# Forgetting attention: one exp over a tile's logits in SBUF, in place, and four PSUM banks for logits in place of two

## The chip, the cores and the metric

The kernel runs on one core of a Trainium2 chip. A core has a matrix engine (PE, which reads SBUF and writes PSUM only), a vector engine (DVE), a scalar engine (ACT), GpSimd (POOL) and a queue that issues DMAs (SP). Each engine takes its instructions in order, and they meet at semaphores. The metric is the device time of one execution, in microseconds. Three runs of the kernel before took 1284.34, 1287.81 and 1289.43 us, the median is 1287.81.

## The reference

Two layers over a sequence of 1024 tokens of 1024 channels. Layer 0 mixes by causal pooling and layer 1 by forgetting attention; both add an attention into 256 memory tokens, gates and an output projection with a layer norm. The part that is changed is the forgetting attention, 16 heads of 64 channels:

```python
logits = einsum('bqhd,bkhd->bhqk', q, k) * 64 ** -0.5
logits = logits + (cum[t] - cum[s])      # cum: running sum of log forget gates
logits = where(s <= t, logits, -inf)
p = softmax(logits, axis=-1)
out = einsum('bhqk,bkhd->bqhd', p, v)
```

`cum[t]` is the same for a whole row, so it cancels in the softmax, and only `cum[s]` has to be added.

## The kernel before, in words

Matrix products that need more precision than one pass of PE gives are made of two or three passes over a high and a low part of each operand. `slab` (line 171) is the workhorse: 128 output channels by 1024 tokens, 48 matmuls of 512 columns into two of three PSUM banks with the tag `pj`, evacuated by ACT and DVE. Its weights come by DMA and are split in two by ACT and DVE, or, while `low[0]` is set, as it is in the forgetting attention, by POOL (lines 146 and 147).

PSUM has eight banks: one for value products (tag `O`), three for slabs (`pj`), two for logits (`L`) and two for transposes (`T`). In the forgetting attention the two `T` banks hold exps.

The forgetting attention is `fox` (line 759). PE's order there is the order of the program text (a manual schedule for PE alone); a scheduler sets the order on DVE, ACT, POOL and SP. For each of the 16 heads it goes through eight tiles of 128 queries, the longest first: tile i has L = 128 (i + 1) keys, in two parts of up to 512 keys where L is over 512, and in one part otherwise. Between a tile's own products PE is given a share of other work, `fill.pump`: the slabs of the next pair of heads and of the gates. One step does this for tile i, the tile before it and the tile five steps back (`LAG`):

- `probs` (line 673): POOL masks the diagonal block of R, the broadcast row of `cum` (line 682, in place; R is loaded once a head). Per part, PE makes two logits passes into an `L` bank (line 688, recorded as line 169), and DVE adds R, writes the result to the tile `p` in SBUF (tag `MK`, four buffers, shared with the value projections) and carries the running minimum along (line 689, a custom instruction and a read of its accumulator). q is stored negated, so the minimum is the softmax's maximum.
- then `behind()` runs `halves` (line 701) of the tile before: DVE adds the parts' sums of exps and scales them (line 706; line 708 for one part) and takes the reciprocal (line 709); per part, ACT writes the high half of the probabilities as fp16 (line 712), and DVE the low half, exp times r less the high half (line 713).
- then the rest of `probs`: per part, ACT takes the exp of `p` into a `T` bank, with its sum (line 695, an ACTIVATE and an accumulator read).
- `turn` (line 718) transposes the halves by a DMA from SP, and five steps later `values` (line 724) multiplies them with the values; ACT and DVE evacuate (lines 738 and 739).

Other work on the same engines in this stage: queries and keys are evacuated by ACT and DVE (lines 627, 628, 638, 639), gates by lines 194 and 195, values by lines 236 to 244, the finished heads are gated by POOL (lines 748 and 756), and in the last pair of heads the output projection's weights are split by ACT and DVE (lines 142 and 143).

Of the kernel before, what the change touches and what calls it, by code (L numbers as in the profile page):

```python
# [9 lines left out]
F32 = mybir.dt.float32  # L10
# [4 lines left out]
AF = mybir.ActivationFunctionType  # L15
ALU = mybir.AluOpType
AX = mybir.AxisListType

P = 128
# [3 lines left out]
ST = S // P  # L23
NH = 512
# [13 lines left out]
PSCALE = 2.0 ** 15  # L38
# [27 lines left out]
def run(units):  # L66
    for _ in units:
        pass
# [3 lines left out]
def trunk_kernel(ctx, tc, x, xT, memT, win, wk, wv0, wv, wmk, wmv, wout, poolw, pscale, lng, lnb, bforget, out):  # L72
# [5 lines left out]
    nc = tc.nc  # L78
# [3 lines left out]
    small = ctx.enter_context(tc.tile_pool(name="small", bufs=4))  # L82
    psum = ctx.enter_context(tc.tile_pool(name="psum", bufs=2, space=bass.MemoryType.PSUM))
# [1 line left out]
        nc.vector.memset(small.tile([P, 8], F32, tag="edge", name="edge"), 0.0)  # L85
    dram = ctx.enter_context(tc.tile_pool(name="dram", bufs=1, space=bass.MemoryType.DRAM))

    count, low = [0], [False]
    since = [0]
    warm = pool.tile([P, NH], BF16, tag="w", name="warm", bufs=6)  # L90
    nc.vector.memset(warm, 0.0)
# [4 lines left out]
    def nm(tag):  # L96
        count[0] += 1
        return f"{tag}{count[0]}"

    def sb(shape, tag, bufs, dt=F32, where=None):  # L100
        return (where or pool).tile(shape, dt, tag=tag, name=nm(tag), bufs=bufs)

    def ps(shape, tag, bufs):
        return psum.tile(shape, F32, tag=tag, name=nm(tag), bufs=bufs)

    def G(shape=(P, S), dt=F32):
        return sb(list(shape), "G", 4, dt)

    def T(shape=(P, S), dt=F32R):
        return sb(list(shape), "T", 6, dt)  # L110
# [10 lines left out]
    def tiny(n, dt=F32):  # L121
        return small.tile([P, n], dt, tag=f"s{n}{dt}", name=nm("s"))
# [330 lines left out]
    y0d = dram.tile([3, P, 4, S], F32, name="y0d")  # L453
    y1d = dram.tile([3, P, 4, S], F32, name="y1d")

    with tc.tile_pool(name="in0", bufs=1) as in0:

        def bt():
            return sb([P, S], "B", 8, F32R, in0)

        def pool_group(g):
            w = WINDOWS[g]
            pms = []
            for f in (2 * g, 2 * g + 1):
                u = sb([P, S], "P", 4)
                run(slab(
                    first[f] if g == 0 else win[0, f], XH, XL, lambda cols, acc: nc.scalar.copy(u[:, cols], acc),
                    ("L", 2) if f == 1 else ("pj", 3),
                ))
                cur, sh = u, 1  # L470
                while sh < w:
                    nxt = G()
                    nc.vector.tensor_tensor(nxt[:, sh:], cur[:, sh:], cur[:, : S - sh], ALU.add)
                    nc.vector.tensor_copy(nxt[:, :sh], cur[:, :sh])
                    cur, sh = nxt, 2 * sh
                pm = G()
                nc.vector.scalar_tensor_tensor(pm[:, w - 1 :], cur[:, w - 1 :], 1.0 / w, u[:, w - 1 :], ALU.mult, ALU.subtract)
                nc.vector.tensor_tensor(pm[:, : w - 1], cur[:, : w - 1], invc[:, : w - 1], ALU.mult)
                nc.vector.tensor_tensor(pm[:, : w - 1], pm[:, : w - 1], u[:, : w - 1], ALU.subtract)
                ph, pl = T(), T()  # L480
                hi_lo(ph, pl, pm)
                pms.append((ph, pl))
            r = raw([P, 2, 2 * P])
            nc.sync.dma_start(r, poolw[g])
            wh, wl = (MK([P, 2, 2 * P]) for _ in range(2))
            hi_lo(wh, wl, r)
            ys = []
            for f in (2 * g, 2 * g + 1):
                y = sb([P, S], "Y", 4, F32, in0)
                run(gate_units(win[0, 12 + f], y, XH, XL))  # L490
                ys.append(y)
            for d in range(2):
                f = 2 * g + d
                for n in range(2):
                    acc = ps([P, NH], "pj", 3)
                    terms = []
                    for ct in range(2):
                        a, b = wh[:, ct, d * P : (d + 1) * P], wl[:, ct, d * P : (d + 1) * P]
                        ph, pl = (t[:, n * NH : (n + 1) * NH] for t in pms[ct])
                        terms += [(a, ph), (a, pl), (b, ph)]  # L500
                    mm3(acc, terms)
                    yn = ys[d][:, n * NH : (n + 1) * NH]
                    nc.vector.scalar_tensor_tensor(yn, acc, pschalf[:, f : f + 1], yn, ALU.mult, ALU.mult)
                nc.sync.dma_start(y0d[f // 4, :, f % 4, :], ys[d])

        pool_group(0)
        kv = mem_kv(0)
        mem_attention(0, XH, XL, kv, bt, lambda: sb([P, S], "Y", 4, F32, in0), y0d[2])
        for g in range(1, 4):
            pool_group(g)  # L510

        XH1, XL1 = (sb([P, KT, S], "A", 2, F32R) for _ in range(2))
        wtags = [("MK", 4)] * 2 + [("W", 4)] * 2 + [("B", 8)] * 4 + [("Y", 4)] * 2 + [("PG", 0), ("w", 0)]
        OutProj(0, w_slots(wtags, in0), y0d).rest(x, XH1, XL1, x1)


    XH, XL = XH1, XL1
    with tc.tile_pool(name="in1", bufs=1) as in1:

        def xy(shape=(P, S)):  # L520
            return sb(list(shape), "B", 10, F32R, in1)
# [148 lines left out]
            nc.sync.dma_start(R, cumd[hd].partition_broadcast(P))  # L670
            return R

        def probs(hd, i, R, sums, behind):

            q, kx, ky = pairs[hd // 2][hd % 2]
            L = (i + 1) * P
            qs = slice(i * P, L)  # L680
            p = MK([P, S], F32)
            nc.gpsimd.affine_select(R[:, qs], R[:, qs], [[-1, P]], ALU.is_ge, -NEG, base=0, channel_multiplier=1)  # L682
            m = tiny(2)
            top = -NEG
            parts = [(0, L)] if L <= NH else [(0, 384), (384, L)] if L == 640 else [(0, NH), (NH, L)]
            for n, (lo, up) in enumerate(parts):
                lg = ps([P, NH], "L", 2)[:, : up - lo]
                mm3(lg, ((q[:, qs], kx[:, lo:up]), (q[:, qs], ky[:, lo:up])))
                nc.vector.tensor_tensor_reduce(p[:, lo:up], lg, R[:, lo:up], 1.0, top, ALU.add, ALU.min, m[:, n : n + 1])  # L689
                top = m[:, n : n + 1]  # L690
            behind()
            es = []
            for n, (lo, up) in enumerate(parts):
                e = ps([P, NH], "T", 2)[:, : up - lo]
                nc.scalar.activation(  # L695
                    e, p[:, lo:up], AF.Exp, bias=top, scale=-1.0, accum_out=sums[:, n, hd % 2, i : i + 1],
                )
                es.append((lo, up, e))
            return hd, i, es, sums

        def halves(hd, i, es, sums):

            L, r = (i + 1) * P, tiny(1)
            one, two = (sums[:, n, hd % 2, i : i + 1] for n in range(2))
            if len(es) == 2:
                nc.vector.tensor_scalar(r, one, two, 1.0 / PSCALE, ALU.add, ALU.mult)
            else:
                nc.vector.tensor_scalar(r, one, 1.0 / PSCALE, None, ALU.mult)
            nc.vector.reciprocal(r, r)
            pair = sb([P, 2 * S], "P", 4, F16)  # L710
            for lo, up, e in es:
                nc.scalar.activation(pair[:, lo:up], e, AF.Copy, scale=r)  # L712
                nc.vector.scalar_tensor_tensor(pair[:, L + lo : L + up], e, r, pair[:, lo:up], ALU.mult, ALU.subtract)  # L713
            return hd, i, pair

        pt = {}
# [42 lines left out]
        def fox(following, out_proj):  # L759
            fill, past, fresh = Fill(), [None] * LAG, [None]  # L760
# [7 lines left out]
            for hd in range(HEADS + 1):  # L768
                pr, b = divmod(hd, 2)
                if hd == HEADS:  # L770
                    fill.add(lead, SLAB)
                if hd < HEADS:
                    if b == 0:
                        o, sums = G(), sb([P, 4 * ST], "sums", 2, F32, small).rearrange("p (n b i) -> p n b i", n=2, b=2)
                        if 0 < pr < 7:
                            fill.add(pair_units(pr + 1), 3 * SLAB)
                        for ahead in {0: (0, 1), 2: (2,), 4: (4,), 7: (7,)}.get(pr, ()):
                            gate_ahead(ahead)
                        if pr == 0:
                            fill.add(following, SLAB)  # L780
                        for late in (3, 5, 6) if pr == 7 else ():
                            fill.add(late_gate(late), SLAB)
                    R, ahead_R = ahead_R, None
                for i in range(ST if hd < HEADS else LAG):
                    tile_of = ST - 1 - i
                    ahead = sum(SHARE[i:]) + (sum(SHARE) if b == 0 else 0)
                    part = fill.left * SHARE[i] / (ahead if hd < HEADS else sum(SHARE[i:LAG]))
                    new, split = None, []

                    def behind():  # L790
                        if fresh[0]:
                            split.append(halves(*fresh[0]))
                            fresh[0] = None
# [7 lines left out]
                            lead = out_proj.early([xy((P, 4, 2 * P)) for _ in range(2)])  # L801
                    if hd < HEADS:
                        new = (hd, tile_of, o)
                        fresh[0] = probs(hd, tile_of, R, sums, behind)
                    else:
                        behind()
                    fill.pump(part * FRAC[0])
                    for what in split:
# [81 lines left out]
```

## Time and profile before

| | us |
|---|---|
| the profiled execution | 1289.07 |
| its span, first to last instruction | 1287.3 |
| PE idle in the span | 35.4 |
| PE waiting for line 689 or 639 before logits (line 169), forgetting attention | 13.4 |
| exps, line 695: 192 activations, and their accumulator reads | 110.8 and 36.4 |
| halves, line 712 on ACT and line 713 on DVE, 192 each | 102.6 and 111.5 |
| logits on DVE, line 689: 128 first parts, as the page lists them | 72.9 |

The page lists the busy time of each engine, then the span in 40 slices, then the chain of work that ended last, then groups of instructions. A group's row has line, engine, operation, output and input with their shapes and the count; then the busy time in us and the mean of one in ns; then the time that the engine sat idle just before these instructions, and what ended most of that. `MK<-L,R` reads: a tile with the tag MK is written from L and R. The table of stretches gives the busy time of each engine between two moments, the clock that PE was granted (1.00 is full) and the share of the DMA engines. The table of waits has who waited, for whom, and total, count and longest.

PE's matmuls overlap and their ends are modelled: a 512-column matmul is listed with 389 to 396 ns, while 24 of them in an undisturbed stretch take 5.44 us.

### The profile page before, as it was taken

How to read it: one execution, taken by the hardware profiler on the slowest of the kernel's cores; microseconds unless marked ns; L12 is line 12 of the kernel's file. 1: busy time of each engine (PE TensorE's matmuls, PEld its weight loads, DVE VectorE, ACT ScalarE, POOL GpSimd, SP SyncE). 2: the span in 40 equal slices, each digit the busy share in tenths (PEclk: the TensorE clock that was granted, in tenths of full speed). 3: DMA queues.
4: the chain of work that ended last, by engine and by line, in shares of the span. 5: the costliest groups of instructions: out<-in, count | busy, mean ns of one | idle time of the engine just before them, and what ended most of it. 6: DMA issues, size and time to landing. Idle time of an engine off the chain costs nothing. (4 is left out here: it accounts for less than half of the span.)

```text
span 1287.3 us, 19678 instructions
## 1 busy us (share of the span) xinstructions
PE 1251.9 (97%) x7018; PEld 1036.6 (81%) x7018; DVE 801.4 (62%) x1905; ACT 579.2 (45%) x1273; POOL 168.8 (13%) x267
## 2 busy tenths in 40 slices
PE   9999999999999999999999999999999999999997
PEld 7888878888778889887887788887888777788885
DVE  6452656355565457267456777777777887674644
ACT  5332642232331124265225667766766776653110
POOL 0000000000000000000003334333334231420000
PEclk9999999999999999999999999999999999999999
DMA  6351343212474226234516866868778786986430
GB/s 221 115 148 50 92 98 114 82 56 91 158 243 137 92 91 183 64 82 112 169 47 157 160 153 162 192 143 172 171 163 185 164 187 155 230 200 200 164 115 33
DMA packets 267426, 178.65 MB, mean 139 GB/s; under 512 B 212288, under 2 KB 225728, under 8 KB 267328
## 3 DMA queue, kind: packets, MB, share of 16 engines
q1 hardware_dynamic: 267328, 177.40, 52.0%
q8 instruction: 55, 0.90, 0.3%
q14 instruction: 43, 0.35, 0.1%
HBM read 94.97 MB, written 22.61 MB: 91 GB/s over the span
## 5 line engine op out<-in xcount | busy, mean ns | idle before, releaser
L181 PE MATMUL pj<-A,w 128*128 128x512 f32 x2928 | 726.5, 396 | 1.0 <-POOL w L147 0.6
L181 PEld LDWEIGHTS pj<-A,w 128*128 128x128 f32 x2928 | 539.5, 189 | 105.8 <-ACT A L142 1.8
L143 DVE TENSOR_TENSOR w<-raw,w 128x512 fp32r<-128x512 f32 x106 | 72.9, 689 | 117.0 <-ACT w L142 115.5
L142 ACT CAST w<-raw 128x512 fp32r<-128x512 f32 x106 | 65.6, 621 | 162.4 <-PE pj L181 103.7
L695 ACT ACTIVATE T<-MK,s 128x512 f32<-128x512 f32 x192 | 110.8, 577 | 56.6 <-DVE s L689 43.3
L713 DVE SCALAR_TENSOR_TENSOR P<-T,s,P 128x512 f16<-128x512 f32 x192 | 111.5, 613 | 34.5 <-ACT P L712 32.9
L712 ACT ACTIVATE P<-T,s 128x512 f16<-128x512 f32 x192 | 102.6, 576 | 48.2 <-issue 20.9
L169 PE MATMUL L<-B,B 128*128 128x512 f32 (+3 forms) x384 | 93.1, 346 | 13.9 <-DVE s L689 11.6
L169 PEld LDWEIGHTS L<-B,B 128*128 128x128 f32 x384 | 70.0, 188 | 36.2 <-DVE s L689 20.9
L689 DVE CUSTOM_DVE_ANT_0 MK<-L,R 128x512 f32<-128x512 f32 (+3 forms) x128 | 72.9, 570 | 15.9 <-PE L L169 10.7
L601 POOL MEMSET G<- 128x128 f32 x1 | 0.2, 205 | 620.3 <-DVE V L324 620.3
L169 PEld LDWEIGHTS <-V 128*128 128x128 f16 x1152 | 65.9, 99 | 17.9 <-issue 17.4
L169 PE MATMUL O<-T,V 128*128 128x128 f16 x1152 | 77.0, 222 | 0.0
L147 POOL TENSOR_TENSOR w<-raw,w 128x512 fp32r<-128x512 f32 x54 | 69.8, 1292 | 3.9
L142 ACT CAST T<-T 128x1024 fp32r<-128x1024 f32 x23 | 24.2, 1051 | 93.4 <-DMA T<-y1d 49.3
L682 POOL TENSOR_SCALAR_AFFINE_SELECT R<-R 128x128 f32<-128x128 f32 x128 | 40.4, 318 | 190.4 <-DVE s L689 107.7
L143 DVE TENSOR_TENSOR T<-T,T 128x1024 fp32r<-128x1024 f32 x23 | 28.1, 1220 | 58.1 <-PE L L358 41.6
L146 POOL TENSOR_SCALAR w<-raw 128x512 fp32r<-128x512 f32 x54 | 36.4, 675 | 143.6 <-PE pj L181 131.7
L213 PE MATMUL pj<-T,w 128*128 128x256 f32 x384 | 48.9, 285 | 2.7 <-ACT w L142 2.1
L213 PEld LDWEIGHTS pj<-T,w 128*128 128x128 f32 x384 | 46.9, 191 | 4.3 <-ACT w L142 2.8
L358 PE MATMUL pj<-B,T 128*128 128x512 f32 x186 | 46.5, 392 | 0.8 <-DVE B L143 0.8
L358 PE MATMUL L<-B,T 128*128 128x512 f32 x174 | 42.5, 389 | 0.0
(212 smaller groups left out, 1599.9 us busy)
## 6 DMA issues: line engine op xcount, KB each, us to landing
raw<-in_win_dram SPq DMA_DIRECT2D x96, 256.0 KB, 2.7
raw<-in_wout_dram SPq DMA_DIRECT2D x48, 256.0 KB, 3.3
B<-B SPq DMA_DIRECT2D x32, 256.0 KB, 3.9
R<-cumd SPq DMA_DIRECT2D x16, 512.0 KB, 4.3
y0d<-Y SPq DMA_DIRECT2D x12, 512.0 KB, 2.7
T<-y0d SPq DMA_DIRECT2D x12, 512.0 KB, 4.3
T<-y1d SPq DMA_DIRECT2D x11, 512.0 KB, 4.5
raw<-in_wmk_dram SPq DMA_DIRECT2D x16, 256.0 KB, 2.7
```

The source lines that it names most:

```text
L142: nc.scalar.copy(hi, src)
L143: nc.vector.tensor_tensor(lo, src, hi.bitcast(F32), ALU.subtract)
L147: nc.gpsimd.tensor_tensor(lo, src, hi.bitcast(F32), ALU.subtract)
L169: nc.tensor.matmul(acc, a, b, start=i == 0, stop=i == len(terms) - 1)
L181: nc.tensor.matmul(accs[n], a[:, k, :], b[:, kt, n * NH : (n + 1) * NH], start=kt == 0 and i == 0, stop=kt == KT - 1 and i == 2,)
L213: nc.tensor.matmul(acc, w[:, k, :], m[pc][:, k, :], start=pc == 0 and k == 0 and i == 0, stop=pc == 1 and k == 3 and i == 2,)
L358: nc.tensor.matmul(accs[a][nh], y[:, k, a * P : (a + 1) * P], w, start=kt == 8 and i == 0, stop=kt == 7 and i == 2,)
L682: nc.gpsimd.affine_select(R[:, qs], R[:, qs], [[-1, P]], ALU.is_ge, -NEG, base=0, channel_multiplier=1)
L689: nc.vector.tensor_tensor_reduce(p[:, lo:up], lg, R[:, lo:up], 1.0, top, ALU.add, ALU.min, m[:, n : n + 1])
L695: nc.scalar.activation(e, p[:, lo:up], AF.Exp, bias=top, scale=-1.0, accum_out=sums[:, n, hd % 2, i : i + 1],)
L712: nc.scalar.activation(pair[:, lo:up], e, AF.Copy, scale=r)
L713: nc.vector.scalar_tensor_tensor(pair[:, L + lo : L + up], e, r, pair[:, lo:up], ALU.mult, ALU.subtract)
```

## The change

Three things change, all in the forgetting attention:

- The PSUM banks of the tags `L` and `T` come from pools of their own. In layer 1 there is one pool of four `L` banks, and what asks for `T` gets `L` too; layer 0 keeps two and two. No bank holds exps any more.
- The exp is taken once for all L keys, from `p` to `p`, in place, with one sum. The halves read `p` in SBUF, still part by part.
- The inverse of the sum (`inverse_of`) is a step of its own, called after the first part of the next tile's logits, ahead of the second part and of the halves.

```diff
     def ps(shape, tag, bufs):
-        return psum.tile(shape, F32, tag=tag, name=nm(tag), bufs=bufs)
+        if tag in ("L", "T") and len(banks) == 2:
+            tag, bufs = "L", 4
+        return (banks[-1] if tag in ("L", "T") else psum).tile(shape, F32, tag=tag, name=nm(tag), bufs=bufs)
...
-    with tc.tile_pool(name="in0", bufs=1) as in0:
+    with tc.tile_pool(name="in0", bufs=1) as in0, tc.tile_pool(name="lt", bufs=2, space=bass.MemoryType.PSUM) as lt:
+        banks.append(lt)
...
-    with tc.tile_pool(name="in1", bufs=1) as in1:
+    with tc.tile_pool(name="in1", bufs=1) as in1, tc.tile_pool(name="ll", bufs=4, space=bass.MemoryType.PSUM) as ll:
+        banks.append(ll)
...
-        def probs(hd, i, R, sums, behind):
+        def probs(hd, i, R, sums, inverse, behind):
...
             for n, (lo, up) in enumerate(parts):
                 lg = ps([P, NH], "L", 2)[:, : up - lo]
                 mm3(lg, ((q[:, qs], kx[:, lo:up]), (q[:, qs], ky[:, lo:up])))
                 nc.vector.tensor_tensor_reduce(p[:, lo:up], lg, R[:, lo:up], 1.0, top, ALU.add, ALU.min, m[:, n : n + 1])
                 top = m[:, n : n + 1]
+                if n == 0:
+                    inverse()
             behind()
-            es = []
-            for n, (lo, up) in enumerate(parts):
-                e = ps([P, NH], "T", 2)[:, : up - lo]
-                nc.scalar.activation(
-                    e, p[:, lo:up], AF.Exp, bias=top, scale=-1.0, accum_out=sums[:, n, hd % 2, i : i + 1],
-                )
-                es.append((lo, up, e))
-            return hd, i, es, sums
+            total = sums[:, hd % 2, i : i + 1]
+            nc.scalar.activation(p[:, :L], p[:, :L], AF.Exp, bias=top, scale=-1.0, accum_out=total)
+            return hd, i, p, total
...
+        def inverse_of(total):
+            r = tiny(1)
+            nc.vector.tensor_scalar(r, total, 1.0 / PSCALE, None, ALU.mult)
             nc.vector.reciprocal(r, r)
+            return r
+
+        def halves(hd, i, p, r):
+            L = (i + 1) * P
             pair = sb([P, 2 * S], "P", 4, F16)
-            for lo, up, e in es:
-                nc.scalar.activation(pair[:, lo:up], e, AF.Copy, scale=r)
-                nc.vector.scalar_tensor_tensor(pair[:, L + lo : L + up], e, r, pair[:, lo:up], ALU.mult, ALU.subtract)
+            for lo, up in parts_of(L):
+                nc.scalar.activation(pair[:, lo:up], p[:, lo:up], AF.Copy, scale=r)
+                nc.vector.scalar_tensor_tensor(pair[:, L + lo : L + up], p[:, lo:up], r, pair[:, lo:up], ALU.mult, ALU.subtract)
...
+                    def inverse():
+                        if fresh[0]:
+                            fresh[0] = (*fresh[0][:3], inverse_of(fresh[0][3]))
```

## The prediction, made before the changed kernel was run

> **What bounds the kernel now.** I read the page first (engines, slices), then the stretch table, then who waited for whom, then the groups with shapes kept apart, then the timeline.
>
> ```profile
> span 1287.3 us, 19678 instructions
> PE 1251.9 (97%) x7018; PEld 1036.6 (81%) x7018; DVE 801.4 (62%) x1905; ACT 579.2 (45%) x1273; POOL 168.8 (13%) x267
> ```
>
> PE is busy 97% of the span, but a busy PE is not PE at its peak. The edit touches only the forgetting attention, whose 128 tiles (16 heads of 8) run from 683 to about 1125 us. The table of stretches has us, busy times, granted clock, DMA:
>
> ```profile
> core 0: us, PE busy (x) PEld busy (x) DVE busy (x) ACT busy (x) POOL busy (x), PEclk, DMA share, GB/s
> 732.00:736.00 4.00, 2.36 (x12) 1.64 (x10) 3.57 (x10) 3.31 (x8) 2.43 (x3) 1.00 0.92 134
> 736.80:740.20 3.40, 3.40 (x16) 2.51 (x15) 2.15 (x5) 0.99 (x3) 0.59 (x2) 0.50 0.87 211
> ...
> 1118.00:1122.00 4.00, 1.24 (x7) 0.77 (x6) 1.81 (x4) 1.89 (x3) 1.83 (x4) 1.00 0.70 239
> 1122.50:1125.90 3.40, 3.40 (x20) 2.65 (x19) 1.49 (x7) 2.38 (x7) 1.53 (x2) 0.50 1.10 223
> 683.00:1125.00 442.00, 427.35 (x2685) 347.62 (x2683) 337.52 (x974) 301.17 (x705) 152.76 (x244) 0.99 0.76 173
> ```
>
> The stage is 442 us: DVE 76% busy, ACT 68%, POOL 35%. After a wait of about 2 us PE runs at half clock for 3.4 us. The waits of PE and of DVE in that stage (total us, times, longest):
>
> ```profile
> PE L L169 <- DVE s L689: 11.6, 13, 2.8
> PE L L169 <- DVE B L639: 1.8, 1, 1.8
> ```
> ```profile
> DVE P L713 <- ACT P L712: 31.7, 58, 4.2
> DVE s L706 <- ACT T L695: 19.5, 18, 1.9
> DVE MK L689 <- PE L L169: 10.4, 16, 1.1
> ...
> DVE s L708 <- ACT T L695: 7.5, 24, 0.5
> ...
> DVE MK L689 <- POOL R L682: 4.6, 8, 2.0
> ```
>
> PE waits for nothing but logits banks that line 689 has not yet read. But DVE waits for PE's logits for only 10.4 us; most of its idle time is waiting for ACT. So **two chains are nearly equal**: PE, and DVE with ACT.
>
> **What PE can gain.** Idle before logits is 11.6 + 1.8 = 13.4 us. It is counted from a matmul's modelled end; from start to start (0.227 us in a steady stream of 512 columns) the trace has 21 such gaps of over 0.15 us, 17 us together. Four times 3.413 us at clock 0.5 lose half each, 6.8 us. Ceiling: 24 us.
>
> The four falls follow waits of 1.97, 2.02, 2.04 (in two pieces) and 2.9 us, while one of 1.8 (at 670 us) has none behind it. The Trainium skill, "TensorE: Matmul & The Clock Gate", section "What's actually happening", has the clock fall after an idle window of about 3.4 us; by it none of these waits would suffice, the 6.8 would not go with them, and the ceiling would be 17. Here the trace decides: 24.
>
> **The change, part by part.**
>
> Four banks: the order of the built programs has PE's instructions in the same places as before. A bank is now needed again four parts later, not two. In this trace PE's need of a bank would then have come at least 3.0 us after line 689 had read the part four before; with two banks that margin is 0.1 us in the 21 gaps. The margin shrinks by the stalls that go (at most 3 to 5 us in a run of heads), so few waits are left while DVE is no slower.
>
> ACT: the rows, and those nearest to the new forms (mean ns):
>
> ```profile
> L713 DVE SCALAR_TENSOR_TENSOR P<-T,s,P 128x256 f16<-128x256 f32 x48 | 22.9, 477 | 3.5 <-ACT P L712 3.2
> L712 ACT ACTIVATE P<-T,s 128x256 f16<-128x256 f32 x48 | 22.5, 469 | 1.9 <-ACT T L695 1.4
> L695 ACT ACTIVATE T<-MK,s 128x512 f32<-128x512 f32 x80 | 55.0, 688 | 45.6 <-DVE s L689 36.6 <-DVE P L713 8.6
> L695 ACT ACTIVATION_READ_ACCUMULATOR T<-MK,s 128x1 f32 x192 | 36.4, 189 | 0.3
> L243 ACT ACTIVATE MK<-MK,s 128x1024 f16<-128x1024 f32 x8 | 9.2, 1147 | 11.3 <-DVE s L240 11.3
> L293 ACT ACTIVATE P<-P,s 128x256 f16<-128x256 f32 x64 | 27.4, 501 | 4.4 <-ACT P L287 2.8 <-DVE s L291 1.5
> L294 DVE SCALAR_TENSOR_TENSOR P<-P,s,P 128x256 f16<-128x256 f32 x64 | 27.2, 479 | 3.8 <-ACT P L293 3.8
> ```
>
> At 1024 keys two exps and two sum reads were 2x688 + 2x189 = 1754 ns; one of each is 1147 + 189 = 1336 (line 243: SBUF to SBUF at 1024). Over 64 two-part tiles: -27 us of ACT. The 192 copies now read SBUF: 501 against 469 at 256, +6 us. ACT goes from 301 to about 280 of 442; hidden, since ACT is no chain by itself, but the DVE behind the exp sees it about 0.4 us sooner.
>
> DVE: the 62 two-part sums at line 706 (212 ns) become the one-part form of line 708 (150 ns): **-4 us**. The subtraction itself costs the same from SBUF (479) as from PSUM (477).
>
> DVE's order: the inverse moves ahead. It is a wait on an in-order queue: behind it stand the tile's second logits part and the subtractions. From the built order I counted, per tile, the DVE work between a tile's last line 689 and its sum, against the exp's time plus 0.2 us. Before, the sums come up 22 us short (measured 27); after 35, since a sum now often stands right behind its own tile's logits. From inverse to subtraction, against a copy's 0.8 us: before 22 short, after 15. Net **+6 us**. Exps no longer wait for banks that the subtraction frees (ACT's wait of line 695 on line 713, 10.9 us): I take **-3**; bounds -10 and +5 for the three together.
>
> The logits tile lives until the subtraction. Of its 128 allocations 113 now follow a subtraction, an earlier instruction of the same queue: nothing, unless a value tile holds two of the four buffers; at worst one tile's 1.6 us six times. No DMA is added or moved past another on SP's queue by more than a place.
>
> The subtraction now has **two inputs in SBUF**. The trace shows what that does beside POOL (timeline, DVE then POOL):
>
> ```profile
> 1147.46 2.01 DVE L143 TENSOR_TENSOR B<-raw,B 128x512 fp32r<-128x512 f32 x1 [0.81 <-ACT B L142]
> 1149.39 0.68 DVE L143 TENSOR_TENSOR w<-raw,w 128x512 fp32r<-128x512 f32 x1
> ```
> ```profile
> 1146.52 2.40 POOL L756 TENSOR_TENSOR R<-R,G 128x1024 f32<-128x1024 f32 x1 [4.28 <-DVE G L195]
> ```
>
> The same instruction takes 0.68 us alone and 2.01 when POOL's began first: it ends 0.6 us after POOL's. Line 713, with one input in PSUM, shows nothing (749 ns alone, 748 beside POOL), though 74 of its 192 began inside a POOL instruction. POOL is busy 35%; weighted by their durations (1292, 660, 319, 740 ns) a running one has 0.44 us left. 192 x 0.35 x 0.44 = 30 us at most by chance; POOL's masks (319 ns) mostly start just after a logits part, when DVE's next is already running, and then POOL waits instead, so I take **+20** (bounds 0 and 30).
>
> **Sum.** DVE's chain: of the 442 us, waits on PE (10.4), on POOL (5.6) and ACT's own waits on PE (14) are give: 412 are its own. 412 - 4 + 6 - 3 + 20 = 431. PE's is 442 - 24 = 418. DVE's is the later, so 11 us go; and PE may run one tile further ahead (442/128 = 3.5 us), which nobody pays at the end, since the value products come five tiles later. Gain 14: the profiled execution, 1289.07 (span 1287.3 and 1.8 around it), becomes 1275. The median of the runs stands 1.3 below it, so I give 1274.
>
> **Rivals.**
> *PE's ceiling* (0.2): hardly any collision, DVE's chain 412, PE's 418 bounds: 1265. For it: DVE is 76% busy. Against: its waits on ACT.
> *The waits only change hands* (0.22): the banks were a symptom; DVE's chain stays near 440 through the sums that wait for their own exps: 1281 to 1294, no sure difference. For it: DVE waits on PE only 10.4 us.
> *Slower, by the port that DVE and POOL share* (0.16): the mean excess of the three collisions in the trace is 0.8 us (1.33, 0.58, 0.55). If the 74 subtractions that begin inside a POOL instruction paid 0.6 each, DVE gains 44 us: 412 - 1 + 44 = 455, 13 over the old stage less 3.5: 1299. It decides from about 34 us added, 78 hits of 0.44. Against: POOL's long instructions (lines 146, 147) come in 52 pairs, not at every tile. The Trainium skill states this rule in "SBUF — State Buffer", section "Who interferes with whom": a DVE instruction with two SBUF inputs and a GpSimd one that reads SBUF exclude each other, the second waits the first out. The trace agrees (2.01 against 0.68).
>
> **How the numbers follow.** Forecast 0.42, 1270 to 1281 by itself. Range 1263 to 1294: low end PE's ceiling, high end the full 30 with ACT's waits 5 longer (412 - 4 + 11 + 30 = 449, +7 less what run-ahead gives back); some 0.05 lies below and 0.13 above. Half a per cent, 6.4 us, is about what a measurement of this kernel tells from none. Faster: 0.2 + 0.42 + 0.02 of the second rival = 0.64; within: 0.21; slower: 0.15.
>
> **What will show it.** PE's wait of line 169 on the logits reduction: under 4 us from 13.4, and no stretch at clock 0.50. The subtraction at 512: from 749 to about 850 ns on average (20/192 us more), long ones only beside POOL. DVE's waits on ACT: copies less, sums more. I am wrong if PE still waits over 8 us for banks, if the subtraction's mean stays at 750 (then 1265), or passes 950 (then slower).

## The result, and the profile after

The changed kernel takes 1300.14 us (median of six runs, 1296.17 to 1301.7), the kernel before 1286.81 (six runs, 1284.33 to 1289.87). The ratio is 1.0097, with a 95% interval of 1.0075 to 1.012: **slower by some 13 us**, where some 14 us faster had been forecast. The profiled execution takes 1300.04, of which the span is 1298.3.

The page of the changed kernel, its first lines:

```profile
span 1298.3 us, 19587 instructions
PE 1252.5 (96%) x7018; PEld 1041.3 (80%) x7018; DVE 818.4 (63%) x1905; ACT 564.2 (43%) x1145; POOL 184.3 (14%) x267
```

ACT has lost 15 us of work, where some 21 had been forecast. DVE and POOL have gained 17 and 15.5, though they run the same number of instructions as before. Next the table of stretches for the window that the forecast used (us; busy time of PE, weight loads, DVE, ACT, POOL; clock; DMA share; GB/s):

```profile
683.00:1125.00 442.00, 419.29 (x2627) 346.00 (x2626) 347.65 (x956) 282.22 (x573) 161.26 (x238) 0.98 0.73 168
```

In the same 442 us PE gets 2627 matmuls done where it did 2685. Who waits for whom there, PE first and then DVE (total us, times, longest):

```profile
PE O L172 <- DVE G L745: 9.3, 9, 1.9
PE pj L184 <- POOL w L149: 7.4, 2, 5.1
PE L L172 <- DVE B L644: 4.0, 1, 4.0
PE pj L184 <- POOL w L150: 1.2, 1, 1.2
PE pj L184 <- DVE B L644: 0.7, 1, 0.7
```
```profile
DVE s L709 <- ACT MK L701: 33.1, 42, 1.3
DVE P L719 <- ACT P L718: 18.4, 50, 0.6
...
DVE MK L695 <- POOL R L688: 5.3, 13, 1.8
...
DVE MK L695 <- PE L L172: 3.6, 5, 1.1
```

Line 695 is the logits reduction (689 before). PE's 11.6 us of waits for it are gone altogether. In their place PE waits for the bank of the value products (O, evacuated by DVE in line 745), for weights that POOL splits and for an evacuation of q: 22.6 us in all, against 14.0. Stretches at half clock take 23.9 us between 670 and 1130 us, against 13.7.

What DVE has more to do is in the groups with shapes kept apart, the subtraction (line 719, 713 before):

```profile
L719 DVE SCALAR_TENSOR_TENSOR P<-MK,s,P 128x512 f16<-128x512 f32 x80 | 69.0, 870 | 9.8 <-ACT P L718 9.5
L719 DVE SCALAR_TENSOR_TENSOR P<-MK,s,P 128x384 f16<-128x384 f32 x48 | 32.4, 675 | 2.9 <-ACT P L718 2.5
L719 DVE SCALAR_TENSOR_TENSOR P<-MK,s,P 128x256 f16<-128x256 f32 x48 | 31.4, 654 | 5.4 <-ACT P L718 5.0
L719 DVE SCALAR_TENSOR_TENSOR P<-MK,s,P 128x128 f16<-128x128 f32 x16 | 7.9, 491 | 4.7 <-ACT P L718 4.7
```

At 256 columns the mean was 477 ns, here it is 654. Over all 192 the two pages have, before and after:

```profile
L713 DVE SCALAR_TENSOR_TENSOR P<-T,s,P 128x512 f16<-128x512 f32 x192 | 111.5, 613 | 34.5 <-ACT P L712 32.9
```
```profile
L719 DVE SCALAR_TENSOR_TENSOR P<-MK,s,P 128x512 f16<-128x512 f32 x192 | 137.3, 735 | 22.8 <-ACT P L718 21.7
```

The mean goes from 613 to 735 ns, that is 192 x 122 = 23.4 us. Sorted by what POOL was doing when each began, at 512 columns: 31 with no POOL instruction beside them take 748 ns, 33 that began inside one take 1031. The timeline of one of these, DVE and then POOL (start, us, instruction; two subtractions of 512 and 384 columns share a row):

```profile
752.10 2.30 DVE L719 SCALAR_TENSOR_TENSOR P<-MK,s,P 128x512 f16<-128x512 f32 x2 [0.26 <-ACT P L718]
```
```profile
751.32 0.62 POOL L149 TENSOR_SCALAR w<-raw 128x512 fp32r<-128x512 f32 x1 [0.57 <-PE pj L184]
752.03 1.30 POOL L150 TENSOR_TENSOR w<-raw,w 128x512 fp32r<-128x512 f32 x1
```

POOL's split began 0.07 us earlier. The two take 2.30 us, where 0.75 + 0.61 = 1.36 would be theirs alone.

The price of one collision can be read off more exactly. Of the 75 subtractions that began inside a POOL instruction, 68 found more than 0.20 us of it left. Each of these took its time alone (748, 612, 477 or 346 ns by width) **plus what POOL had left, less 0.20 us**, to within 0.012 us; the other seven paid under 0.01 us. In the rows above POOL had 1.23 us left, and the first subtraction took 1.78 us in place of 0.75. These collisions add up to 23.1 of the 23.4 us: 17.2 with the low split (line 150), 2.5 with the high one, 2.1 with a single gate of 2.4 us, and only 0.5 with the masks, which have little more than 0.20 us left when a subtraction begins.

POOL is held in turn. Its rows for the masks and the low split, before and then after:

```profile
L682 POOL TENSOR_SCALAR_AFFINE_SELECT R<-R 128x128 f32<-128x128 f32 x128 | 40.4, 318 | 190.4 <-DVE s L689 107.7
L147 POOL TENSOR_TENSOR w<-raw,w 128x512 fp32r<-128x512 f32 x54 | 69.8, 1292 | 3.9
```

```profile
L688 POOL TENSOR_SCALAR_AFFINE_SELECT R<-R 128x128 f32<-128x128 f32 x128 | 51.2, 404 | 225.2 <-DVE s L695 117.1
...
L150 POOL TENSOR_TENSOR w<-raw,w 128x512 fp32r<-128x512 f32 x54 | 73.1, 1354 | 3.8
```

### The profile page after: what moved, and what is told of

Read it like the earlier page. It is cut to its first block, busy times and chain, and to the rows that moved or that the text cites. A ratio compares the mean times of both kernels' runs of the same rounds, so it can differ in the third digit from the quotient of the medians.

```text
span 1298.3 us, 19587 instructions
## 1 busy us (share of the span) xinstructions
PE 1252.5 (96%) x7018; PEld 1041.3 (80%) x7018; DVE 818.4 (63%) x1905; ACT 564.2 (43%) x1145; POOL 184.3 (14%) x267
## 5 line engine op out<-in xcount | busy, mean ns | idle before, releaser
L719 DVE SCALAR_TENSOR_TENSOR P<-MK,s,P 128x512 f16<-128x512 f32 x192 | 137.3, 735 | 22.8 <-ACT P L718 21.7
L701 ACT ACTIVATE MK<-MK,s 128x1024 f32<-128x1024 f32 (+7 forms) x128 | 99.3, 775 | 106.1 <-DVE s L695 91.0
L718 ACT ACTIVATE P<-MK,s 128x512 f16<-128x512 f32 x192 | 108.8, 606 | 23.8 <-ACT MK L701 11.6
L172 PE MATMUL L<-B,B 128*128 128x512 f32 (+3 forms) x384 | 89.3, 341 | 4.0 <-DVE B L644 4.0
L172 PE MATMUL O<-T,V 128*128 128x128 f16 x1152 | 77.9, 223 | 11.1 <-DVE G L745 11.0
L172 PEld LDWEIGHTS L<-B,B 128*128 128x128 f32 x384 | 72.3, 190 | 19.4 <-DVE B L644 4.4
L688 POOL TENSOR_SCALAR_AFFINE_SELECT R<-R 128x128 f32<-128x128 f32 x128 | 51.2, 404 | 225.2 <-DVE s L695 117.1
L150 POOL TENSOR_TENSOR w<-raw,w 128x512 fp32r<-128x512 f32 x54 | 73.1, 1354 | 3.8
L361 PE MATMUL L<-B,T 128*128 128x512 f32 x204 | 50.0, 389 | 0.0
```

The costliest lines, as they stand in the source:

```text
L150: nc.gpsimd.tensor_tensor(lo, src, hi.bitcast(F32), ALU.subtract)
L172: nc.tensor.matmul(acc, a, b, start=i == 0, stop=i == len(terms) - 1)
L361: nc.tensor.matmul(accs[a][nh], y[:, k, a * P : (a + 1) * P], w, start=kt == 8 and i == 0, stop=kt == 7 and i == 2,)
L701: nc.scalar.activation(p[:, :L], p[:, :L], AF.Exp, bias=top, scale=-1.0, accum_out=total)
L718: nc.scalar.activation(pair[:, lo:up], p[:, lo:up], AF.Copy, scale=r)
L719: nc.vector.scalar_tensor_tensor(pair[:, L + lo : L + up], p[:, lo:up], r, pair[:, lo:up], ALU.mult, ALU.subtract)
```

## The experiments

**Theory S**: the subtraction, now with two operands in SBUF, waits for POOL; this makes DVE late, and PE pays for it wherever DVE is what it waits for. Rivals: **I**, the inverse moved ahead makes DVE wait for an exp that isn't done; **O**, the single bank O is the next bound, whatever POOL does. Each ratio below is against the kernel before on the same chip (medians 1282.8 to 1285.7).

### Early inverse alone, late inverse alone

To the kernel before, only the early inverse is added:

```diff
                 top = m[:, n : n + 1]
+                if n == 0:
+                    inverse()
```

> The kernel before with one part of the change alone: the inverse is taken after the first part of the next tile's logits; the exps stay in two PSUM banks, two logits banks. Theory S (the subtraction with two SBUF inputs waits for POOL, which makes DVE's chain later): no second SBUF input here, so within 5 us of the kernel before (1287), and the subtraction at 512 columns stays at 749 ns. Rival I (the early inverse makes DVE wait for its own tile's exp: waits of the sums 34 us against 27): 1295 to 1302.

Measured: 1281.26, ratio 0.9989 (0.9974 to 1.0004). Then the changed kernel with the inverse put back behind the logits:

```diff
-                if n == 0:
-                    inverse()
+            inverse()
             behind()
```

> The changed kernel with the inverse put back ahead of the halves, behind both logits parts; exp in place in SBUF and four logits banks stay. Theory S: the subtractions still lose 20 to 25 us to POOL, so 1296 to 1304. Rival I: back to 1287 or below.

Measured: 1297.39, ratio 1.011 (1.0079 to 1.014). The loss stays without the early inverse and does not come with it: rival I falls.

### POOL's splits left out

One pair of split weights is kept and used for every slab in the stage, so that POOL has its masks and gates only. The other weights are still loaded, but not split and not multiplied. The same is done to the kernel before, as a control.

```diff
     def split_w(src_dram, shape):
         r = raw(shape)
         nc.sync.dma_start(r, src_dram)
+        if low[0]:
+            return kept
...
             run(start_units(own, following))
+            kept.extend(split_w(win[1, 0, 0], [P, 4, P]))
             low[0] = True
```

> The changed kernel without POOL's splits of weights in the forgetting attention: the weights are still loaded, but every slab of that stage multiplies with one pair that was split ahead of it (this leaves out part of the computation). 100 of POOL's 153 us in the stage go. Theory S: the subtractions lose about 6 us in place of 23, DVE catches up, and it is 5 to 15 us below its own control, the kernel before without the splits. Rival I and rival O (one bank for the value products is what PE waits for, whatever POOL does): 5 to 12 us above the control.

> Control for the one before: the kernel before without POOL's splits of weights in the forgetting attention, in the same way (this leaves out part of the computation). Its subtraction reads PSUM and does not meet POOL, so all theories expect little: 1280 to 1288, PE's waits for logits banks still 8 us or more.

Measured: 1281.87 (0.9999, 0.998 to 1.0018) and 1288.27 (1.0042, 1.0025 to 1.0058). The control lies just above the 1280 to 1288 that were expected. With POOL's splits the change costs 13 us; without them it gains 6.4, within the 5 to 15 of theory S. The subtraction's row of the first of these (the two numbers after the bar are us in all and mean ns):

```profile
L723 DVE SCALAR_TENSOR_TENSOR P<-MK,s,P 128x512 f16<-128x512 f32 x192 | 117.7, 634 | 27.0 <-ACT P L722 25.9
```

The weights are still loaded, but no slab of the stage waits for its own weights any more, and POOL's queue is shorter in every respect, so this does not yet show that it is the holding.

### The subtraction's operand

The changed kernel with three banks for logits; the subtraction reads the fourth bank, zeroed once, in place of the exps.

```diff
-            tag, bufs = "L", 4
+            tag, bufs = "L", 3
...
-                nc.vector.scalar_tensor_tensor(pair[:, L + lo : L + up], p[:, lo:up], r, pair[:, lo:up], ALU.mult, ALU.subtract)
+                nc.vector.scalar_tensor_tensor(pair[:, L + lo : L + up], zero[0][:, : up - lo], r, pair[:, lo:up], ALU.mult, ALU.subtract)
```

> The changed kernel with three banks for logits, where the subtraction reads its first operand from the fourth bank, zeroed once, in place of the exps in SBUF; everything else, the copies and the waits for them too, stays. It leaves out part of the computation: the low half of the exps is not theirs. Theory S (two SBUF operands make the subtraction wait for POOL, which makes DVE late): the subtraction's sum falls from 141 us to 116-121, and the time lies at least 12 us below its control e6, at 1274-1287. Theory O (the single bank O and the order of the queues bind, whatever the subtraction takes): the sum may fall, but the time stays within 4 us of the control. Theory C (what the subtraction pays is its wait for ACT's copy): no change in the time, since those waits stay.

The control has the three banks and the real operand.

> The control of e5 and e8: the changed kernel with three banks for logits and the fourth left idle. Theory S: DVE is late by tens of microseconds' worth of its own work, one bank changes little: 1297-1306, the subtraction's sum 138-143 us. Theory B (four banks let PE run ahead, past the values' bank, and this is what costs): it falls by a third or more of the loss, to 1287-1296.

Measured: 1282.56 (0.9973, 0.9959 to 0.9987) against 1298.4 (1.0098, 1.0077 to 1.0119). The groups of the first, at 512 columns:

```profile
L719 DVE SCALAR_TENSOR_TENSOR P<-Z,s,P 128x512 f16<-128x512 f32 x80 | 59.3, 748 | 9.6 <-ACT P L718 9.4
```

74 of its 192 subtractions still began inside a POOL instruction, and cost nothing more (748 ns inside and outside). **One operand's place is worth 15.8 us**, as S said; O and C fall. The subtraction also no longer reads the tile `p`, which therefore comes free earlier; this can hardly be it, since in the changed kernel only 0.2 us of DVE's waits before logits are put down to the subtraction. Three banks do as well as four, so theory B of the control falls too.

### Two banks for logits

Without the lines that map the tag T to L, two banks for logits are left and the other two lie idle.

```diff
-        if tag in ("L", "T") and len(banks) == 2:
-            tag, bufs = "L", 4
```

> The changed kernel with two banks for logits as before, the other two left idle in the attention; exps in SBUF, in place. Theory S: the subtraction's sum stays at 138-143 us, DVE stays late, and PE now waits for it at the logits' banks: 1300-1318, no less than the changed kernel. Theory B (the four banks cause the loss): back to 1281-1291.

Measured: 1305.51 (1.0164, 1.0149 to 1.018). The waits of PE in the window of the stage:

```profile
PE L L170 <- DVE s L693: 19.4, 27, 2.7
PE L L170 <- DVE B L642: 3.2, 1, 3.2
```

So the exp in place, with the early inverse but without further banks, costs about 21 us (1.64%), and the further banks give some 7 to 8 back (1.0164 to about 1.0098). Theory B is wrong: the banks help. The time lies where S had it, but the subtraction's sum does not: 149 us (192 x 777 ns) against 138 to 143 expected and 141 in the changed kernel. So in these two profiles the subtraction alone differs by the 8 us that the banks give back.

### A second bank for value products

Three banks for logits, and the fourth shares the value products with O.

```diff
-            acc = ps([P, 2 * P], "O", 1)
+            acc = ps([P, 2 * P], "O" if c % 2 == 0 else "Z", 1)
```

> The changed kernel with three banks for logits and the fourth as a second bank for the value products, used in turn with O. Theory O (the single bank O is what binds after the change): the 9.3 us of PE's waits for O's evacuation go and the time falls by 8-14 us below the control e6. Theory S (O is only where DVE's lateness is charged): those waits go, but come back as waits for logits, the evacuation of q and the weights; the time falls by 0-6 us, the subtraction's sum stays at 138-143 us.

Measured: 1296.95 (1.0094, 1.0077 to 1.0111), 1.5 below its control. PE's waits in the stage:

```profile
PE L L172 <- DVE s L695: 11.5, 11, 2.7
PE pj L184 <- POOL w L149: 4.1, 2, 2.7
PE L L172 <- DVE B L644: 4.0, 1, 4.0
```

No wait for O's evacuation is left. But the control, with three banks for logits and one for O, has few of them already:

```profile
PE L L172 <- DVE s L695: 11.1, 12, 2.8
PE O L172 <- DVE G L745: 2.0, 6, 0.7
```

So it was the fourth bank for logits, not the second one for values, that moved the waits: with four banks PE waits 9.3 us at O and none at logits, with three 2.0 and 11.1, with two none and 19.4. Four and three banks take the same time. Which bank PE waits at is mostly where DVE's lateness is charged.

### The first part's exp in PSUM

Three banks for logits and one for the exps of a tile's first part. The second part stays in SBUF, in place.

```diff
+                e = p[:, lo:up] if n else ps([P, NH], "Z", 1)[:, : up - lo]
+                total = sums[:, n, hd % 2, i : i + 1]
+                nc.scalar.activation(e, p[:, lo:up], AF.Exp, bias=top, scale=-1.0, accum_out=total)
```

> A mixed form: three banks for logits, the fourth for the exps of a tile's first part (at most 512 columns), which the copy and the subtraction read from there; the second part, where there is one, stays in SBUF, in place. So 128 of the 192 subtractions read one operand from PSUM and 64 read two from SBUF. Two exps on the larger tiles again, the reciprocal early. Theory S: the subtraction's sum lies at 123-131 us, between the 118 and the 141, and the time with it, at 1281-1291, at least 8 us below the changed kernel. Theory Q (what costs is the order of the queues that one exp for each tile brings, in place or not): 1291 or less only because two exps are back; told apart by the subtraction's sum, which would stay above 135 or not move with the time.

Measured: 1297.3 (1.0101, 1.0067 to 1.0134). The subtraction's sum is 122 us, just under the 123 to 131 expected, but **the time is not**: 6 us above the range. DVE's longest waits, from the first to the last logits:

```profile
DVE P L727 <- ACT P L726: 47.3, 69, 1.4
DVE s L717 <- ACT Z L704: 17.3, 33, 0.9
DVE s L715 <- ACT MK L704: 7.5, 9, 1.6
DVE s L715 <- ACT Z L704: 6.8, 12, 2.5
```

Over that whole stretch DVE waits 90.8 us for ACT, where it waited 78.5 in the kernel before. With two banks for logits and two for exps, as the kernel before has them (the edit is shown against the mixed form):

```diff
-                e = p[:, lo:up] if n else ps([P, NH], "Z", 1)[:, : up - lo]
+                e = p[:, lo:up] if n else ps([P, NH], "T", 2)[:, : up - lo]
```

> The mixed form again (the first part's exp in PSUM, the second part's in SBUF, in place; the reciprocal early), now with two banks for logits and two for the exps. 64 of 192 subtractions read two SBUF operands. If the single bank for exps made the loss of the mixed form (DVE waited 79 us for ACT there, 62 in the kernel before): those waits fall to 58-68 us, and the time to 1282-1290, with a sum of the subtraction of 120-127. If the 64 subtractions from SBUF alone are enough to make DVE late: 1292 or more.

Measured: 1285.04 (1.0016, 1.0001 to 1.0031), the subtraction's sum 124 us, DVE's waits for ACT 81.7 us over the whole stretch. The 62 and 79 in the expectation were sums of the longest rows for sums and subtractions only; in that measure it is 59 here, at the low end of what was expected. Most of the mixed form's loss was the one bank, at which exp, copy and subtraction of neighbouring tiles had to take turns; it went although the banks for logits fell from three to two. 7 us more of subtraction alone cost next to nothing.

### A memset for the subtraction

Four banks, and nothing for the subtraction to read or to wait for.

```diff
-                nc.vector.scalar_tensor_tensor(pair[:, L + lo : L + up], p[:, lo:up], r, pair[:, lo:up], ALU.mult, ALU.subtract)
+                nc.vector.memset(pair[:, L + lo : L + up], 0.0)
```

> The changed kernel (four banks) with a memset of the low half in place of the subtraction: no operand to read, no wait for ACT's copy. It leaves out part of the computation: the low half of the exps is zero. It asks what became of the 24 us that the forecast took for PE's waits and clock falls. If DVE's chain is what PE waits for (O, q, the weights and the logits alike): the time comes near to the forecast's ceiling for PE, 1262-1272. If the waits belong to the shape of the kernel whatever DVE takes (the single bank O, the weights by way of POOL, the DMAs): 1275-1285, as with the subtraction from PSUM.

Measured: 1277.72 (0.9949, 0.9933 to 0.9965). DVE's work falls by 70 us against the kernel before, and still only 8 us go. PE's waits:

```profile
PE pj L184 <- POOL w L149: 8.7, 2, 4.6
PE L L172 <- DVE B L644: 2.0, 1, 2.0
```

The longest of them in the timelines of PE, POOL and SP (the queue that issues DMAs):

```profile
1092.55 3.01 PE L184 MATMUL pj<-A,w 128*128 128x512 f32 x5 [4.59 <-POOL w L149]
```
```profile
1091.88 0.62 POOL L149 TENSOR_SCALAR w<-raw 128x512 fp32r<-128x512 f32 x1 [2.47 <-DMA raw<-in_win_dram]
```
```profile
1086.25 0.34 SPq L756 DMA_DIRECT2D y1d<-G  x1
1086.69 1.37 SPq L728 DMA_TRANSPOSE T<-P  x1
1088.15 0.53 SPq L154 DMA_DIRECT2D raw<-in_win_dram  x1
```

POOL waits for the weights' load, and the load stood on SP's queue behind a transpose and a store of the last pair of heads. In these rows no bank has a part. The kernel before has only 0.6 us of such waits (for line 147); why weights come later in the changed one was not taken apart.

### Smaller doses of POOL

The high half of the splits made by ACT:

```diff
-        nc.gpsimd.tensor_scalar(hi, src, 1.0, 1.0, ALU.mult, ALU.mult)
+        nc.scalar.copy(hi, src)
```

> The changed kernel with the high half of each weight split made by ACT in place of POOL in the attention stage (the low half stays on POOL): 37 of POOL's some 180 us go, ACT gets some 33 us more (54 at 0.62 us). A smaller dose of the missing splits. Theory S: the subtractions that begin inside a POOL instruction fall from 75 to 58-70, their sum from 141 to 134-140 us, the time by 2-8 us below the changed kernel, 1291-1298. Theory A (ACT's chain is as tight as DVE's): above 1302, with more waits of DVE for ACT's exp and copy.

Measured: 1303.55 (1.0152, 1.0118 to 1.0185). The subtraction's sum did as S said (135 us; 47 began inside a POOL instruction, fewer than the 58 to 70 expected); the time went the other way. PE's waits in the stage, and ACT's timeline at the longest of them:

```profile
PE pj L184 <- ACT w L149: 10.5, 2, 5.6
PE O L172 <- DVE G L745: 7.3, 7, 1.6
```
```profile
1094.59 0.62 ACT L149 CAST w<-raw 128x512 fp32r<-128x512 f32 x1 [4.15 <-DMA raw<-in_win_dram]
1095.11 1.04 ACT L701 ACTIVATE MK<-MK,s 128x896 f32<-128x896 f32 x1
```

The split now stands on ACT's queue: it waits 4.15 us for its load, and an exp waits behind it. DVE waits 85.4 us for ACT (80.0 in the changed kernel), and half clock takes 34 us. Theory A had the direction.

Then the same work on POOL, in four pieces, and its control:

```diff
+        for k in range(4):
+            nc.gpsimd.tensor_scalar(hi[:, k, :], src[:, k, :], 1.0, 1.0, ALU.mult, ALU.mult)
+            nc.gpsimd.tensor_tensor(lo[:, k, :], src[:, k, :], hi[:, k, :].bitcast(F32), ALU.subtract)
```

> The changed kernel with each of POOL's two weight splits made in four pieces of 128 columns: the same work in the same places of POOL's queue, but a piece holds a quarter as long (some 0.33 us for 1.29). Theory S (a subtraction with two SBUF operands waits until the POOL instruction that began before it ends): the subtraction's extra, 23 us, falls by a third to two thirds, to a sum of 125-134 us, and the time by 4-12 us against the changed kernel, to 1288-1296; POOL's own work grows somewhat, and the weights with it, which bounds the gain. Theory Q (how the queues fall together, not the holding): sum and time stay, or the time rises with POOL's longer work, 1299-1306.

> The control: the kernel before with the same pieces. Both theories: its subtraction reads PSUM and stays at 117-118 us; the time stays within 1283-1292, since POOL has room and only the weights come some 0.5 us later.

Measured: 1295.77 (1.0105, 1.0088 to 1.0122) and 1287.53 (1.0039, 1.0024 to 1.0054). The page of the first:

```profile
L720 DVE SCALAR_TENSOR_TENSOR P<-MK,s,P 128x512 f16<-128x512 f32 x192 | 126.1, 677 | 28.1 <-ACT P L719 27.0
L151 POOL TENSOR_TENSOR w<-raw,w 128x128 fp32r<-128x128 f32 x216 | 109.1, 526 | 3.6
```

The extra of the subtraction falls to half: (677 - 613) x 192 = 12.3 us. Against its control the change costs 8.2 us in place of 13.3; the intervals of the two overlap, so the times alone would not decide. The collisions do: here too each of the 81 subtractions that found more than 0.20 us of a POOL instruction left paid what was left less 0.20 us, to within 0.014. The holding by POOL is what counts, not only the order. But nothing is won against the kernel before, since the pieces keep POOL busy for 184 us where the whole splits took 110, and DVE's waits for POOL grow from 5.3 to 11.9 us. With the second value bank added:

> A candidate: POOL's splits in pieces, three banks for logits, and the fourth as a second bank for value products. Theory S: the subtraction's sum 125-134 us as in the pieces alone, and 0-6 us less than the pieces alone, as the second bank gave: 1283-1293. Theory Q: 1295-1300, as with the second value bank alone.

Measured: 1293.57 (1.0086, 1.0068 to 1.0105), just above its range and no repair either. Of the kernels that compute all, the early inverse alone is the best: below the changed kernel, and level with the one before.

## Why the prediction was wrong

The likeliest case fell and the third rival, the port that DVE and POOL share, came true, at its time (1299) but not by its arithmetic. One number goes with the time of the slow kernels: DVE's **own time**, its busy time and its waits for ACT and POOL, from the first to the last logits matmul. It is added up from the table of stretches and the table of waits of each kernel. The stretches of the two main kernels, before and after:

```profile
684.70:1158.20 473.50, 458.85 (x2881) 373.60 (x2880) 360.28 (x1028) 320.48 (x747) 161.70 (x254) 0.99 0.77 175
```
```profile
687.60:1169.30 481.70, 457.22 (x2880) 377.28 (x2879) 377.28 (x1028) 305.82 (x619) 177.19 (x254) 0.98 0.73 172
```

DVE is busy for 360.3 and 377.3 us, and its waits for ACT and POOL add up to 78.5 + 5.6 and 80.0 + 5.3. Each row of the table is one profiled execution, while the ratio is of all runs.

| kernel | ratio | subtraction, mean ns | DVE's own, us | stage, us |
|---|---|---|---|---|
| memset | 0.9949 | - | 402.8 | 462.6 |
| early inverse alone | 0.9989 | 612 | 439.8 | 464.6 |
| operand in PSUM | 0.9973 | 614 | 443.3 | 466.6 |
| before | 1 | 613 | 444.4 | 473.5 |
| changed, without POOL's splits | 0.9999 | 634 | 446.1 | 470.1 |
| mixed, two banks for exps | 1.0016 | 648 | 446.4 | 471.8 |
| mixed, one bank | 1.0101 | 636 | 458.3 | 478.8 |
| changed, pieces | 1.0105 | 677 | 460.8 | 481.0 |
| changed | 1.0097 | 735 | 462.6 | 481.8 |
| changed, three banks | 1.0098 | 742 | 464.0 | 484.0 |
| changed, two banks | 1.0164 | 777 | 471.2 | 489.9 |

From 457 us on, the stage is DVE's own time and 17 to 23 us more, in every kernel run, those left out of the table included. Between 439 and 450 it is 23 to 30 us more, in no clear order. Below that it stops following: 37 us less of DVE (memset against the early inverse) give 2 us.

- **PE's ceiling: wrong, 24 us counted and 11 there.** With DVE far out of the way (memset), the stage shortens from 473.5 to 462.6, and the median of the whole kernel by 8. The rest is in the last pair of heads, where weights come late by way of SP and POOL: two waits, 8.7 us together, and half clock behind them.
- **Four banks: the mechanism right, its worth not.** PE's waits for the reduction are gone. But the forecast asked only whether a logits bank would be free, not what else PE waits for from a late DVE: bank O, q's evacuation, weights. They took over. The waits before already said so: of the 13.4 us, 1.8 were a wait for q's evacuation (line 639) and not for a bank, and 0.6 us of waiting for split weights (line 147) stood beside them.
- **ACT: right in direction, too large.** 301 to 282 us looks like the 280 of the forecast, but in the same 442 us the changed kernel gets less done. From the first to the last logits ACT falls from 320.5 to 305.8, by 15 us where -27 and +6 make -21. The copies cost 6.2 us more (102.6 to 108.8), forecast 6. Nothing hangs on it: hidden, as said.
- **DVE's order and sums: right.** The sums fell to 148 ns. DVE's waits for ACT went from 78.5 to 80.0 us, where +6 and -3 were forecast.
- **The subtraction beside POOL: right in size, and partly by luck.** +20 forecast, +23.4 measured; at 512 columns 870 ns, forecast about 850. The forecast charged all that POOL has left, 0.44 us on average, and took a third off for the masks; measured is 0.20 us less than what is left at each collision, which makes the masks nearly free and leaves the long splits as the cost. The Trainium skill's rule in "SBUF — State Buffer", section "Who interferes with whom", cited with the third rival, holds here in both directions: 748 against 1031 ns on DVE, 318 against 404 for POOL's masks. By the trace the later instruction does not lose the whole of what is left, but 0.20 us less.
- **The sum: this is the step that failed.** "DVE's chain: of the 442 us, waits on PE (10.4), on POOL (5.6) and ACT's own waits on PE (14) are give: 412 are its own." The change of DVE's own time was forecast well, 412 to 431, that is +19; measured are 444.4 to 462.6, +18.2 (this measure counts the waits for POOL in, and unnamed gaps out). But not all 30 us of give were to be had. In the forecast's own three rows, over the same 442 us, the changed kernel still has 18 of the 30: DVE waits 3.6 us on PE and 5.3 on POOL, and ACT 9.4 on PE (without a wait of 10.1 that ended at 685 us, before the first tile). Before, the stage exceeds DVE's own time by 29 us; in the changed kernel by 19, and in no run by less than 17. Beside its own time, DVE waits there for PE (3.6 us) and for DMAs (2.7), and has gaps of some 12 us in which no row names a releaser. So about 10 us were slack, not 30. Of the 18 added, 10 were absorbed and 8.3 lengthened the stage; the profiled span grew by 11.0, of which 2.9 lie ahead of the first logits. There the changed kernel has a stretch at half clock (674.9 to 678.3 us) that the kernel before has not, which costs 1.7 of them. By the medians the kernel lost 13 us, so the slack may have been less than 10.
- **The run-ahead of 3.5 us** was not seen.
- **The third rival** asked 0.6 us of each of the 74 collisions, 44 us in all, and set the turning point at 34 us added. It was 0.3 each, and the turning point lies near 10. Both its numbers were too large, and their errors cancelled: that its time came out at 1299 is luck.
- **The upper end of the range** took +11 for ACT's waits, where the bounds given above it allow less. With 1294 it lay below what came.
- **What was to show it**: PE's wait for the reduction under 4 us came true, and still the kernel is slower. PE does wait over 8 us for a bank, but for O (9.3), of which the forecast had not thought. "No stretch at clock 0.50" was wrong, and so was the mark of 950 ns: 870 were enough.

What stays open: why the kernel before, with 444 us of DVE's own time, has a stage 7 us longer than the one that reads its operand from PSUM with 443. Its waits at two logits banks are a possible cause, but the early inverse alone has the same two banks, 440 us of own time and a stage of 464.6. A part is the execution that was profiled: 1289.07 us, where the medians of this kernel are 1282.8 to 1287.8, while the other was profiled at 1281.88 with a median of 1282.56. No run takes this apart.

## What to carry to other kernels

Slack is not the idle time of an engine. Ask how much of the idle time has ever been used up by a kernel like this one, and take only the rest as cover. When a wait at one buffer is removed and the late engine stays late, look for every other place at which it is waited for. And an operand moved from PSUM to SBUF is to be priced by what POOL does beside it, on both engines: here each collision cost what POOL had left, less 0.20 us, so long POOL instructions made nearly all of the price.

## What the runs showed of the hardware that had not been expected

**Half clock comes by windows.** The forecast had it follow a wait of about 2 us. In the records of the granted clock every stretch at 0.50 in the attention starts a whole number of 3.413 us from the others of its run, in all 17 kernels. Counted on that grid, the falls of the two main kernels follow windows in which PE is listed busy for 0.08 to 0.55 of the time; windows at 0.52 and 0.57 were followed by none. So the length of one wait does not decide: the same wait of 1.65 us, for line 597 (602 after), which ended at 673.1 us in the changed kernel and at 671.8 in the one before, was followed by half clock in the former alone. The busy share of a window is only a rough sign as well. The two groups overlap, and elsewhere windows at 0.45 and 0.47 (late inverse, pieces) were followed by none. What exactly is counted stays open. The Trainium skill, "TensorE: Matmul & The Clock Gate", section "What's actually happening", has a window of 3413 ns that runs on by itself, and lets the clock fall after an idle one. The grid agrees with the window; but here windows that PE is listed busy for up to about half of the time sufficed.

**Cutting POOL's instructions in four kept POOL busy half as long again.** In the control the low split takes 463 ns for a quarter, where the whole takes 1292, and the high split 315, where the whole takes 675. Neighbouring pieces overlap a little, so the busy times are the fair measure: 95.3 + 64.0 us in place of 69.8 + 36.4, that is 50% more, in a kernel whose subtraction does not hold POOL up.

**The first 0.20 us of a subtraction ran beside POOL.** This is what the 68 collisions of the changed kernel have in common, and the 81 of the pieces: the instruction began, and lost only what POOL still had left after 0.20 us.
